# A rotary embedding on one core: all of x loaded early as fp16, with rows of 8 KB instead of 4 KB in loads and stores

## The chip, the cores and the metric

One core of a Trainium2 chip. The metric is the device time of one execution in microseconds, read as a median of several runs. "Span" is the time from the first to the last instruction in a profile; the device time is 1.7 to 2.2 us longer. All times inside a run are counted from the first instruction of its span.

## The reference

```python
# x: (8, 8, 1024, 64) float32; freqs: 32; positions: 0..1023; scale: 0.5
angles = np.outer(positions * scale, freqs)          # (1024, 32)
cos, sin = np.cos(angles), np.sin(angles)
x_first, x_second = x[..., :32], x[..., 32:]
out = concatenate([x_first * cos - x_second * sin,
                   x_first * sin + x_second * cos], axis=-1)   # float32
```

16.8 MB are read and 16.8 MB written, all as float32. Inside the kernels x, the tables and the results are fp16, except for the first unit's x and the set-up, which are fp32.

## The kernel before

The 64 heads are cut into 16 units of 4 heads (1 MB in HBM). In a unit, two heads fill the 128 partitions (64 partitions each, 16 positions in a partition), twice. So one partition's piece is 16 x 64 floats: a row of 4 KB in HBM.

```python
PAIRS_PER_UNIT = 2; PREFETCH = 5; BUF_X = 7; BUF_O = 7; BUF_P = 3
HP = P // 2;  K = S // HP;  KD = K * D          # 64, 16, 1024

def unit_dram(t, u):
    return t.rearrange("(i r) n -> i (r n)", r=2)[
        u * PU : (u + 1) * PU, :].rearrange("i (p n) -> p i n", n=KD)

X0 = xin0.tile([P, PU, KD], FP32)
nc.sync.dma_start(out=X0, in_=unit_dram(xv, 0))          # the first unit, not cast
for u in (0, 1):
    nc.sync.dma_start(out=pos_i64[u * HP : (u + 1) * HP, :], in_=...)
...
def load_unit(u):                                        # fp32 in HBM -> fp16 in SBUF
    X = xin.tile([P, PU, KD], FP16, tag="X")
    nc.gpsimd.dma_start(out=X, in_=unit_dram(xv, u))
for u in range(1, min(1 + PREFETCH, NU)):
    load_unit(u)
...                                                      # set-up: tables of cos and sin, 128 x 512
for u in range(NU):
    if u + 1 + PREFETCH < NU:
        load_unit(u + 1 + PREFETCH)
    nc.vector.tensor_tensor(out=pc, in0=X, in1=cosT, op=ALU.mult)    # 128 x 2048
    nc.vector.tensor_tensor(out=ps, in0=X, in1=sinT, op=ALU.mult)
    nc.vector.tensor_tensor(out=ov_[:, :, 0:half], in0=pcv[:, :, 0:half],
                            in1=psv[:, :, half:D], op=ALU.subtract)  # 128 x 1024
    nc.vector.tensor_tensor(out=ov_[:, :, half:D], in0=psv[:, :, 0:half],
                            in1=pcv[:, :, half:D], op=ALU.add)
    nc.gpsimd.dma_start(out=unit_dram(ov, u), in_=OUT)   # fp16 in SBUF -> fp32 in HBM
```

## Time and profile before

| | before |
|---|---|
| device time, median (3 runs) | 87.17 us (87.07 to 87.43) |
| span of the profiled run | 85.4 us |
| busiest engine | VectorE, 61.4 us (72%) |
| rows moved by the GpSimd queue | 7,936 and 496 end records |
| DMAs issued by GpSimd | 15 loads, 16 stores |

How to read it: VectorE's share is an average over a kernel in which it neither starts first nor ends last. A row is one contiguous piece in HBM that one of the 16 DMA engines moves; an end record is the 4-byte record that each engine moves after its rows of one DMA. The line to read first is that of the DMA, and its GB/s count the destination's bytes, so a casting load shows half of what it reads. The prediction below shows these lines.

### The profile page before, as it was taken

To read this page: it belongs to the slowest core of one execution; us is meant where nothing else is said; L and a number is where in the kernel's file an instruction comes from. 1 tells how busy PE (TensorE), PEld (TensorE's weight loads), DVE (VectorE), ACT (ScalarE), POOL (GpSimd) and SP (SyncE) were. 2 spreads that over 40 slices of the span, in tenths; PEclk is the share of its full clock that TensorE was granted. 3 is DMA by queue.
4 is the path that set the end of the run, shared out by engine and by line. 5 is a ranking of instruction groups with operands and counts; after the bars stand their busy time and mean duration, and the time that the engine had idled before them with its cause. 6 is when DMAs were issued, how large, how long until landed. Compare 5 with 4: busy or idle time off the path is not lost.

```text
span 85.4 us, 193 instructions
## 1 busy us (share of the span) xinstructions
PE 0.6 (1%) x2; PEld 0.5 (1%) x2; DVE 61.4 (72%) x72; ACT 3.5 (4%) x5; POOL 22.6 (26%) x35
## 2 busy tenths in 40 slices
PE   0002000000000000000000000000000000000000
PEld 0002000000000000000000000000000000000000
DVE  0002979999999999999999999999995992000000
ACT  6000090000000000000000000000000000000000
POOL 4990000005306245063360630311303033000000
DMA  2799999999999999999999999999999999999960
GB/s 19 313 288 214 208 211 213 212 208 211 257 384 218 421 430 271 319 351 257 415 208 396 274 334 338 252 407 221 406 260 331 426 428 428 428 426 416 424 225 0
DMA packets 8867, 25.72 MB, mean 301 GB/s; under 512 B 674, under 2 KB 674, under 8 KB 8866
## 3 DMA queue, kind: packets, MB, share of 16 engines
q0 software_dynamic: 8432, 24.64, 107.0%
q1 hardware_dynamic: 434, 1.07, 3.7%
q14 instruction: 1, 0.01, 0.0%
HBM read 16.79 MB, written 16.78 MB: 393 GB/s over the span
## 4 chain that ended last, share of the span: by engine, by line
DVE 46%; issue 23%; DMA 7%; POOL 4%; ACT 1%; SPq 1%; POOLq 1%; DVEq 0%
DVE ps L139 16%; DVE pc L138 11%; DVE OUT L144 8%; DVE OUT L148 8%; DMA pos_i<-in_positions_dram 7%; POOL out_dram L153 4%; ACT tabs L120 1%; DVE m L114 1%; POOLq L184 1%; DVE y L102 1%; DVE rneg L116 1%; SPq L76 1%; SPq L71 1%; DVE yc L109 1%; DVE posf L97 0%
## 5 line engine op out<-in xcount | busy, mean ns | idle before, releaser
L153 POOL DMA_DIRECT2D out_dram<-OUT x16 | 11.5, 718 | 47.8 <-DVE OUT L148 47.8
L138 DVE TENSOR_TENSOR pc<-X,tabs 128x2048 f16<-128x2048 f16 (+1 forms) x16 | 20.5, 1284 | 1.6 <-DMA X<-in_x_dram 1.0
L139 DVE TENSOR_TENSOR ps<-X,tabs 128x2048 f16<-128x2048 f16 (+1 forms) x16 | 20.5, 1284 | 0.0
L90 POOL DMA_DIRECT2D X<-in_x_dram x15 | 10.9, 739 | 1.2 <-POOLq L170 0.8
L144 DVE TENSOR_TENSOR OUT<-pc,ps 128x1024 f16<-128x1024 f16 x16 | 10.9, 684 | 0.0
L148 DVE TENSOR_TENSOR OUT<-ps,pc 128x1024 f16<-128x1024 f16 x16 | 10.9, 683 | 0.0
L97 DVE CAST posf<-pos_i 128x16 f32<-128x16 int32 x1 | 0.2, 174 | 6.9 <-DMA pos_i<-in_positions_dram 6.9
L120 ACT ACTIVATE tabs<-rneg 128x512 f16<-128x512 f32 x4 | 2.2, 617 | 8.7 <-DVE rneg L116 8.7
L120 ACT ACT_TABLE_LOAD x1 | 1.3, 1283 | 0.7 <-PEq L170 0.7
L102 DVE TENSOR_TENSOR y<-posf,cfreq 128x512 f32<-128x512 f32 x1 | 0.7, 687 | 0.1
L84 DVE MEMSET coef<- 1x128 f32 x1 | 0.2, 165 | 0.8 <-PEq L170 0.8
L116 DVE SCALAR_TENSOR_TENSOR rneg<-m,yc 128x512 f32<-128x512 f32 x1 | 0.7, 685 | 0.0
L116 DVE SCALAR_TENSOR_TENSOR rneg<-m,y 128x512 f32<-128x512 f32 x1 | 0.7, 684 | 0.0
L86 PE MATMUL cfreq<-freq_row,coef 1*128 1x32 f32 x2 | 0.6, 391 | 7.3 <-DMA freq_row<-in_freqs_dram 7.3
L86 PEld LDWEIGHTS cfreq<-freq_row,coef 1*128 1x128 f32 x2 | 0.5, 304 | 7.3 <-issue 7.3
L114 DVE TENSOR_SCALAR m<-yc 128x512 f32<-128x512 f32 x1 | 0.4, 427 | 0.0
L109 DVE TENSOR_SCALAR yc<-y 128x512 f32<-128x512 f32 x1 | 0.4, 426 | 0.0
L114 DVE TENSOR_SCALAR m<-y 128x512 f32<-128x512 f32 x1 | 0.4, 422 | 0.0
L170 POOL MEMSET const-float32-0.0<- 128x1 f32 x1 | 0.1, 93 | 0.2 <-issue 0.2
L170 POOL MEMSET const-bfloat16-1.0<- 128x1 bf16 x1 | 0.1, 95 | 0.0
L170 POOL MEMSET const-float32-1.0<- 128x1 f32 x1 | 0.1, 93 | 0.0
L170 POOL MEMSET const-uint8-127<- 128x1 uint8 x1 | 0.1, 92 | 0.0
## 6 DMA issues: line engine op xcount, KB each, us to landing
out_dram<-OUT POOLq DMA_DIRECT2D x16, 1024.0 KB, 13.2
X<-in_x_dram POOLq DMA_DIRECT2D x15, 512.0 KB, 12.3
X<-in_x_dram SPq DMA_DIRECT2D x1, 1024.0 KB, 5.1
pos_i<-in_positions_dram SPq DMA_DIRECT2D x2, 8.0 KB, 5.3
freq_row<-in_freqs_dram SPq DMA_DIRECT2D x1, 0.1 KB
```

Source lines behind the costliest of these rows:

```text
L86: nc.tensor.matmul(out=cfreq, lhsT=coef, rhs=freq_row, start=True, stop=True)
L90: nc.gpsimd.dma_start(out=X, in_=unit_dram(xv, u))
L102: nc.vector.tensor_tensor(out=y, in0=posf.unsqueeze(2).broadcast_to((P, K, half)), in1=cfreq.unsqueeze(1).broadcast_to((P, K, half)), op=A ...
L109: nc.vector.tensor_scalar(out=yc, in0=y, scalar1=0.25, scalar2=None, op0=ALU.add)
L114: nc.vector.tensor_scalar(out=m, in0=src, scalar1=_MAGIC, scalar2=None, op0=ALU.add)
L116: nc.vector.scalar_tensor_tensor(out=rneg, in0=m, scalar=_MAGIC, in1=src, op0=ALU.subtract, op1=ALU.subtract)
L120: nc.scalar.activation(out=tabs[:, i, :, h * half : (h + 1) * half], in_=rneg, func=AF.Sin, bias=0.0, scale=-_TWO_PI_DN,)
L138: nc.vector.tensor_tensor(out=pc, in0=X, in1=cosT, op=ALU.mult)
L139: nc.vector.tensor_tensor(out=ps, in0=X, in1=sinT, op=ALU.mult)
L144: nc.vector.tensor_tensor(out=ov_[:, :, 0:half], in0=pcv[:, :, 0:half], in1=psv[:, :, half:D], op=ALU.subtract,)
L148: nc.vector.tensor_tensor(out=ov_[:, :, half:D], in0=psv[:, :, 0:half], in1=pcv[:, :, half:D], op=ALU.add,)
L153: nc.gpsimd.dma_start(out=unit_dram(ov, u), in_=OUT)
```

## The change

Its intent: longer rows (fewer, larger pieces for the DMA), loads out of the way of the stores (all of x stays in SBUF as fp16), fewer DMAs. The arithmetic of a unit is the same.

```diff
-PAIRS_PER_UNIT = 2; PREFETCH = 5; BUF_X = 7; BUF_O = 7
+GROUPS = (1, 1, 2, 2, 3, 3, 3)
+BUF_O = 10
-    HP = P // 2
+    HEADS = 4
+    HP = P // HEADS                       # 32 positions per partition: rows of 8 KB
     K = S // HP
+    xv = x.rearrange("b h s d -> (b h s d)").rearrange("(u p n) -> p u n", p=P, n=N)
-        nc.sync.dma_start(out=pos_i64[...], ...)          # two
+        nc.scalar.dma_start(out=pos_i64[...], ...)        # four
-    for u in range(1, min(1 + PREFETCH, NU)):
-        load_unit(u)                                      # the others inside the loop
+    for g, n in enumerate(GROUPS):
+        X = xin.tile([P, n, N], FP16, name=f"X{g + 1}")
+        nc.gpsimd.dma_start(out=X, in_=xv[:, u0 : u0 + n, :])
-    tabs = consts.tile([P, 2, K, D], FP16)                # both halves written, 4 activations
+    cosT = consts.tile([P, K, half], FP16)                # one half, 2 activations,
+    sinT = consts.tile([P, K, half], FP16)                # read twice by a broadcast:
+    cos_b = cosT.unsqueeze(2).broadcast_to((P, K, 2, half))
+    sin_b = sinT.unsqueeze(2).broadcast_to((P, K, 2, half))
 ...
-        nc.gpsimd.dma_start(out=unit_dram(ov, u), in_=OUT)
+        nc.gpsimd.dma_start(out=ov[:, u, :], in_=OUT.rearrange("p k h j -> p (k h j)"))
```

## The prediction

> **What bounds the kernel now.** I read the page first (busy shares, slices, queues), then the stage windows, then the groups by shape, the waits, the order of time, and last the DMA records of the trace one by one.
>
> ```profile
> DVE  0002979999999999999999999999995992000000
> DMA  2799999999999999999999999999999999999960
> GB/s 19 313 288 214 208 211 213 212 208 211 257 384 218 421 430 271 319 351 257 415 208 396 274 334 338 252 407 221 406 260 331 426 428 428 428 426 416 424 225 0
> ...
> q0 software_dynamic: 8432, 24.64, 107.0%
> ...
> HBM read 16.79 MB, written 16.78 MB: 393 GB/s over the span
> ```
>
> VectorE has the largest busy share of the engines (72%), but it stops seven slices before the end. The DMA row is at 9 from the third slice to the 38th. The GB/s row counts the bytes on the destination side: a casting load lands half the bytes that it reads, so 211 there is 422 at HBM, and the stores show 426 to 428 directly. On the HBM side the rate is therefore the same, some 420 to 430, in load, mixed and store slices. That is the mark of a DMA bound kernel. The windows show its edges:
>
> ```profile
> 1.20:2.40 1.20, 0.00 (x0) 0.00 (x0) 0.00 (x0) 0.82 (x1) 1.13 (x2) 1.00 0.41 34
> 4.80:20.00 15.20, 0.60 (x2) 0.49 (x2) 11.37 (x14) 2.19 (x4) 2.34 (x4) 1.00 1.13 215
> 20.00:62.00 42.00, 0.00 (x0) 0.00 (x0) 42.00 (x49) 0.00 (x0) 14.38 (x20) 1.00 1.19 321
> 62.00:82.00 20.00, 0.00 (x0) 0.00 (x0) 7.88 (x10) 0.00 (x0) 2.15 (x3) 1.00 1.23 398
> 82.00:82.30 0.30, 0.00 (x0) 0.00 (x0) 0.00 (x0) 0.00 (x0) 0.00 (x0) 1.00 0.76 232
> 82.30:85.40 3.10, 0.00 (x0) 0.00 (x0) 0.00 (x0) 0.00 (x0) 0.00 (x0) 1.00 0.03 8
> ```
>
> The last two columns are DMA share and GB/s. The time has three parts: 2.4 us before the first load is at full rate, 79.9 us of full DMA (2.4 to 82.3), and 3.1 us of completion and closing. The median time of 87.17 is 1.8 us above the 85.4 span; I carry that 1.8 over.
>
> VectorE's work by shape, and the waits:
>
> ```profile
> L139 DVE TENSOR_TENSOR ps<-X,tabs 128x2048 f16<-128x2048 f16 x15 | 18.3, 1217 | 0.0
> L144 DVE TENSOR_TENSOR OUT<-pc,ps 128x1024 f16<-128x1024 f16 x16 | 10.9, 684 | 0.0
> L138 DVE TENSOR_TENSOR pc<-X,tabs 128x2048 f16<-128x2048 f32 x1 | 2.3, 2292 | 0.6 <-ACT tabs L120 0.6
> POOL out_dram L153 <- DVE OUT L148: 47.8, 16, 12.6
> DVE posf L97 <- DMA pos_i<-in_positions_dram: 6.9, 1, 6.9
> DVE pc L138 <- DMA X<-in_x_dram: 1.0, 1, 1.0
> ```
>
> In the order of time a unit takes 3.47 us (neighbours overlap, so less than 2 x 1.217 + 2 x 0.684). The 47.8 us that GpSimd waits for VectorE cost nothing: the DMA queue has work meanwhile. The last store is issued here:
>
> ```profile
> 71.19 0.72 POOL L153 DMA_DIRECT2D out_dram<-OUT  x1 [1.75 <-DVE OUT L148]
> ```
>
> In the DMA records the sixteenth store's first row moves only at 79.14 us, so it stood 8 us in the queue. VectorE has that much slack.
>
> **The DMA's cost of one row.** Taking all differences between start times of rows, one spacing stands out. In the store stage it is 153 ns (then 306, 459, 612), for 4 KB rows to HBM; in the load stage 154 ns (308, 462, 616); for the fp32 load from SyncE about 155.5. After every 16 rows of one DMA there is a 4-byte record, and spacings across it are 21 ns longer. So a unit's load costs 16 x 0.154 + 0.021 = 2.485 us and a store 16 x 0.153 + 0.021 = 2.469 us; the unit starts in the records show 2.48 and 2.47. Sum for the kernel: first load 16 x 0.1555 = 2.49, 15 loads 37.27, 16 stores 39.50, small constants 0.2, together 79.46 of the 79.9 us found. The rest is ramp and engines that end unevenly.
>
> **What the Trainium skill says.**
> (1) DMA: Bandwidth & Descriptors, "Where 436 GB/s comes from": the ceiling is 16 ports x 32 bytes x 850 MHz = 435 GB/s, and it says that for transfers with HBM its other limit, about 358, binds. The trace differs: 428 in store slices, so the first ceiling is the one met. At it, 4096 bytes are 128 beats or 150.6 ns; the 153 and 154 ns of the trace are 130 and 131 beats.
> (2) The same page, "Why small descriptors are slow (HBM only)": a fixed overhead of about 3 cycles for each packet, its example being a 256-byte descriptor. The 2 to 3 cycles that I find at 4 KB agree. This is what longer rows can save, so it is small.
> (3) The same page, "Issuing engines are not separate DMA queues": all DMAs run on the same 16 engines and interleave. The trace agrees (one total rate throughout), so moving the position loads to ScalarE and the order of loads and stores create no bandwidth.
> (4) Vector Engine (DVE) Microarchitecture Reference, "5.1 Performance modes": two elements per cycle need 16-bit operands with innermost step 1; a row read again and again with step 0 was tried and kept that rate. The trace has it for a broadcast of the outer dimension (1.217 us for 2048, against 2.29 with fp32) and for runs of 32 (0.684 for 1024), not yet for a broadcast in the middle.
>
> **The change part by part.**
> *Rows of 8 KB.* If the 2 and 3 cycles are paid once for each row, an 8 KB store row takes 256 + 2 cycles = 303.5 ns and a load row 256 + 3 = 304.7. A store becomes 8 x 0.3035 + 0.021 = 2.449, sixteen 39.18 (0.32 less). Loads: 15 units x 8 x 0.3047 = 36.56, and seven end records instead of fifteen, 0.15, together 36.71 (0.56 less). The first load 8 x 0.306 = 2.45 (0.04 less). Sum: **0.92 us off the DMA stage**, all of it on the path.
>
> *All loads early.* Seven GpSimd issues at 0.73 us each (now seven as well in the first 6.4 us). In the trace the queue serves loads and stores in order of issue (the first store moves at 22.08 us, after the seven loads ahead of it), so all loads go first, until about 2.4 + 2.45 + 36.7 = 41.6 us, then stores back to back. No byte is removed. The one load wait (1.0 us) goes, off the path: 0.
>
> *Set-up on VectorE and ScalarE.* 32 positions per partition instead of 16, so every table operation doubles to 128x1024: at one cycle per element the 0.69 us ones become 0.69 + 512/0.96 = 1.22, the 0.43 ones 0.43 + 256/0.96 = 0.69, an activation from 0.617 to about 1.04 (two instead of four). The chain from positions to first product grows from 4.0 us (7.84 to 11.88) to about 0.2 + 3 x 1.22 + 3 x 0.69 = 5.9. Positions on their own ScalarE queue should not stand behind all of the first load, which may return 1 to 3 us. First product between 10 and 14 us, then two fp32 products 4.4 + 1.2, then 15 x 3.47 = 52: VectorE ends at 68 to 72 us. Its sixteenth store is wanted at about 41.6 + 15 x 2.45 = 78.4. Off the path: 0.
>
> *Ten output buffers.* Unit 11 needs store 1 landed: about 41.6 + 2.45 + 2 = 46, while VectorE gets there at some 16 + 9 x 3.47 + 2 = 49 at the earliest. Later units only gain margin (2.45 against 3.47). When loads end, eight or so stores are queued, 20 us of work, and VectorE adds one each 3.47 us, so the queue lasts the eight remaining ones. No stall: 0.
>
> Sum: DMA ends at 82.3 - 0.9 = 81.4, span 84.5, time 87.17 - 0.9 = **86.3 us**, 1.0% less.
>
> **The rivals.**
> A. *Rows are cut at 4 KB inside the DMA*, so the overhead is paid as often as now. Then only eight end records go, 8 x 21 ns = 0.17 us: 87.0. No row of 8 KB of x is in this trace, so nothing speaks against it.
> B. *The overhead is hidden at 8 KB*, and the ceiling is met. Each engine moves 2.10 MB at 27.2 bytes per ns (the skill's ceiling / 16, an estimate) in 77.1 us, plus 0.5 of end records and 0.2 of constants: 77.8 instead of 79.46, so 85.5. Even this is 1.9% only, which is why I give "faster" little.
> C. *The middle broadcast loses the doubled rate.* A product then takes some 2.2 us, a unit 5.6, VectorE ends near 13 + 16 x 5.6 = 103, and the time is about 109, bound by VectorE. Against: the skill's note and the runs of 32 at 684 ns.
> D. *The start slips or engines end unevenly*: longer issues of 384 rows, or a queue that can't hold 1,920 rows at once. GpSimd works 5 us ahead of need, and landing times of up to 18.4 us (18.4 / 2.47 x 256 = some 1,900 rows) show that as many were held before. At worst some 1 us: 87 to 88.
>
> **Range and chances.** The sum gives 86.3; A and B bracket it at 87.0 and 85.5; the spread of before is 0.36. D widens the upper end. Range **85.3 to 87.4**. Faster by over 2% means below 85.43, beyond even B: 0.12. Slower by over 2% (above 88.9) needs C or a strong D: 0.07. Within 2%: 0.81.
>
> **What would show it.** Right: row spacings of about 303 to 305 ns in the DMA records (A: 306 to 308; B: 301); stores at 428 to 431 GB/s; slices at half of that until about 41 us and full after; products still at 1.217 us; GpSimd never waiting so long that the DMA row drops below 9 between 3 and 81 us; 3.1 us of closing. Wrong: a hole in the DMA row about 41 to 50 us (stores late), products at 2.2 us (C), or rows of 8 KB at another rate than these cycles, which would mean that I read a property of one row length as a cost of each row.

## The result, and the profile after

The changed kernel took 86.0 us (median of 4 runs, 85.94 to 86.14) beside 87.3 for before (87.07 to 87.72). The ratio is 0.986, 95% interval 0.982 to 0.990. A ratio here is the mean time of one kernel's runs over that of the other's of the same rounds, so it is not quite the ratio of the medians. Run again later with five rounds it was 0.984. So: 1.4 to 1.6% faster, 86.3 predicted.

First the page of the changed kernel: the slices of VectorE and DMA, the GpSimd queue, and the HBM bytes.

```profile
DVE  0000799999999999999999999999999999300000
DMA  2899999999999999999999999999999999999970
GB/s 31 331 280 212 212 216 216 216 210 216 216 214 210 216 216 216 212 214 218 171 418 432 436 424 412 432 432 428 428 428 436 420 412 436 436 424 432 428 284 0
...
q0 software_dynamic: 4336, 24.64, 99.1%
...
HBM read 16.81 MB, written 16.78 MB: 399 GB/s over the span
```

The same bytes move in half the rows (4,336 records are 3,968 rows and 368 end records, against 8,432). The row of GB/s has lost its alternation: half-value slices (loads) up to the twentieth, then full ones (stores). The DMA row still stands at 9 from the third to the 38th slice. One slice is low, 171, at the change from loads to stores.

Then the windows of the changed kernel (the last two columns are DMA share and GB/s):

```profile
1.20:2.40 1.20, 0.00 (x0) 0.00 (x0) 0.00 (x0) 0.00 (x0) 1.16 (x2) 1.00 0.64 102
4.80:20.00 15.20, 0.60 (x2) 0.50 (x2) 11.19 (x11) 2.11 (x2) 1.30 (x2) 1.00 1.06 214
20.00:40.00 20.00, 0.00 (x0) 0.00 (x0) 20.00 (x24) 0.00 (x0) 3.28 (x6) 1.00 1.07 215
40.00:42.00 2.00, 0.00 (x0) 0.00 (x0) 2.00 (x4) 0.00 (x0) 0.00 (x0) 1.00 1.06 174
42.00:60.00 18.00, 0.00 (x0) 0.00 (x0) 18.00 (x22) 0.00 (x0) 2.95 (x6) 1.00 1.12 426
60.00:80.00 20.00, 0.00 (x0) 0.00 (x0) 12.27 (x15) 0.00 (x0) 2.38 (x5) 1.00 1.12 428
81.50:84.20 2.70, 0.00 (x0) 0.00 (x0) 0.00 (x0) 0.00 (x0) 0.00 (x0) 1.00 0.02 6
```

VectorE's groups by shape, a wait, and the last store's issue in the order of time:

```profile
L128 DVE TENSOR_TENSOR pc<-X,cosT 128x2048 f16<-128x2048 f16 x15 | 18.2, 1216 | 0.0
L132 DVE TENSOR_TENSOR OUT<-pc,ps 128x1024 f16<-128x1024 f16 x16 | 10.9, 681 | 0.0
...
DVE posf L90 <- DMA pos_i<-in_positions_dram: 7.0, 1, 7.0
...
72.60 0.53 POOL L138 DMA_DIRECT2D out_dram<-OUT  x1 [1.93 <-DVE OUT L135]
```

The product with a broadcast in the middle takes 1,216 ns, as the one without did (1,217). VectorE now ends later than before, its last store issued at 72.60 instead of 71.19 us, and the kernel ends sooner. That is what "not the bound" looks like.

Where the 1.3 us went, by the two traces. The start and end of the DMA's work are taken from its records, row by row:

| | before | after | difference |
|---|---|---|---|
| first row of the GpSimd queue starts | 5.05 | 4.95 | -0.10 |
| from there to the end of the last row | 77.89 | 77.17 | -0.72 |
| from there to the end of the span | 2.44 | 2.10 | -0.34 |
| device time less span (means of the runs) | 1.94 | 1.77 | -0.17 |

In sum -1.33. The first line is about as large as its scatter (4.88 to 5.00 in six traces of kernels with this start). The third is far beyond its own (2.10 to 2.14 in the six traces with 23 GpSimd DMAs, 2.42 to 2.49 in the five with 31). The spans of before vary (84.9 to 86.0 in later runs), so that the sum holds for these two traces and not for every pair of runs. The windows show the ends, in before and then in the changed kernel (rows count where they start):

```profile
82.50:83.00 0.50, 0.00 (x0) 0.00 (x0) 0.00 (x0) 0.00 (x0) 0.00 (x0) 1.00 0.09 25
83.00:84.00 1.00, 0.00 (x0) 0.00 (x0) 0.00 (x0) 0.00 (x0) 0.00 (x0) 1.00 0.00 0
```
```profile
81.60:82.00 0.40, 0.00 (x0) 0.00 (x0) 0.00 (x0) 0.00 (x0) 0.00 (x0) 1.00 0.14 41
82.00:83.00 1.00, 0.00 (x0) 0.00 (x0) 0.00 (x0) 0.00 (x0) 0.00 (x0) 1.00 0.00 0
```

### The profile page after: what moved, and what is told of

Read it like the earlier page. It is cut to its first block, busy times and chain, and to the rows that moved or that the text cites. A ratio compares the mean times of both kernels' runs of the same rounds, so it can differ in the third digit from the quotient of the medians.

```text
span 84.2 us, 183 instructions
## 1 busy us (share of the span) xinstructions
PE 0.6 (1%) x2; PEld 0.5 (1%) x2; DVE 63.6 (76%) x72; ACT 3.4 (4%) x3; POOL 13.7 (16%) x27
## 3 DMA queue, kind: packets, MB, share of 16 engines
q0 software_dynamic: 4336, 24.64, 99.1%
## 4 chain that ended last, share of the span: by engine, by line
DMA 45%; issue 31%; POOL 10%; POOLq 1%
DMA X<-in_x_dram 45%; POOL out_dram L138 5%; POOL X L78 5%; POOLq L169 1%; POOLq L138 0%; POOLq L155 0%
## 5 line engine op out<-in xcount | busy, mean ns | idle before, releaser
L129 DVE TENSOR_TENSOR ps<-X,sinT 128x2048 f16<-128x2048 f16 (+1 forms) x16 | 20.5, 1282 | 0.0
L128 DVE TENSOR_TENSOR pc<-X,cosT 128x2048 f16<-128x2048 f16 (+1 forms) x16 | 20.4, 1282 | 0.0
L138 POOL DMA_DIRECT2D out_dram<-OUT x16 | 8.6, 538 | 58.4 <-DVE OUT L135 55.5
L78 POOL DMA_DIRECT2D X<-in_x_dram x7 | 4.9, 715 | 0.8 <-POOLq L155 0.8
L95 DVE TENSOR_TENSOR y<-posf,cfreq 128x1024 f32<-128x1024 f32 x1 | 1.2, 1220 | 0.8 <-PE cfreq L87 0.8
L119 ACT ACTIVATE sinT<-rnegs 128x1024 f16<-128x1024 f32 x1 | 1.1, 1057 | 8.8 <-DVE rnegs L109 8.8
L109 DVE SCALAR_TENSOR_TENSOR rnegs<-ms,y 128x1024 f32<-128x1024 f32 x1 | 1.2, 1219 | 0.0
L109 DVE SCALAR_TENSOR_TENSOR rnegc<-mc,yc 128x1024 f32<-128x1024 f32 x1 | 1.2, 1217 | 0.0
L117 ACT ACTIVATE cosT<-rnegc 128x1024 f16<-128x1024 f32 x1 | 1.1, 1057 | 0.1
L115 DVE TENSOR_SCALAR yc<-y 128x1024 f32<-128x1024 f32 x1 | 0.7, 693 | 0.0
```

What stands on the lines that cost most here:

```text
L78: nc.gpsimd.dma_start(out=X, in_=xv[:, u0 : u0 + n, :])
L95: nc.vector.tensor_tensor(out=y, in0=posf.unsqueeze(2).broadcast_to((P, K, half)), in1=cfreq.unsqueeze(1).broadcast_to((P, K, half)), op=A ...
L109: nc.vector.scalar_tensor_tensor(out=rneg, in0=m, scalar=_MAGIC, in1=src, op0=ALU.subtract, op1=ALU.subtract)
L117: nc.scalar.activation(out=cosT, in_=rc, func=AF.Sin, bias=0.0, scale=-_TWO_PI_DN)
L119: nc.scalar.activation(out=sinT, in_=rs, func=AF.Sin, bias=0.0, scale=-_TWO_PI_DN)
L128: nc.vector.tensor_tensor(out=pc, in0=X, in1=cos_b, op=ALU.mult)
```

## The experiments

The theory: the kernel is bound by the DMA, which pays 3.5 ns for each load row and 2.4 ns for each store row beside the bytes, so longer rows pay; loading early and VectorE's changes lie off the path. Rivals: the gain comes from the order (all loads before all stores); from the number of DMAs; or VectorE is nearer to the path than it looks.

### 1. Rows of 8 KB alone: rows8_inter

```diff
-    HP = P // 2
+    HP = P // 4                # and r=4, PAIRS_PER_UNIT = 1; all else as before
```

> The kernel before with the rows alone changed to 8 KB (4 heads in one set of rows, so 32 positions per partition and a doubled set-up); loads still one unit each, five ahead, mixed with the stores. Row theory (2 to 3 cycles per row, 21 ns per end record): loads 15 x (8 x 0.3047 + 0.021) = 36.88 instead of 37.27, stores 0.32 less, first load 0.04 less: 0.75 us below before, and up to 0.25 more if the first load's faster issue starts the DMA earlier. So a ratio to before of 0.989 to 0.991. Order theory (the gain comes from all loads going first): ratio 1.00.

Measured: 89.15 us, ratio 1.024 (1.021 to 1.027), slower by 2%. Both theories missed it. The DMA and GB/s rows of this kernel's page show why, and so do its windows:

```profile
DMA  1899999999279999999999999999999999999960
GB/s 23 342 273 212 214 212 210 214 212 210 56 301 301 259 425 412 199 400 265 344 323 282 381 233 427 226 402 269 336 329 276 432 425 432 447 421 421 428 229 0
...
21.00:22.00 1.00, 0.00 (x0) 0.00 (x0) 1.00 (x2) 0.00 (x0) 0.00 (x0) 1.00 1.03 209
22.00:23.00 1.00, 0.00 (x0) 0.00 (x0) 1.00 (x3) 0.00 (x0) 0.00 (x0) 1.00 0.37 70
23.00:24.00 1.00, 0.00 (x0) 0.00 (x0) 1.00 (x2) 0.00 (x0) 0.42 (x1) 1.00 0.00 0
24.00:25.00 1.00, 0.00 (x0) 0.00 (x0) 1.00 (x2) 0.00 (x0) 0.40 (x2) 1.00 0.45 180
```

In the eleventh slice the DMA has nothing to do. Seven loads were queued at the start (seven buffers) and they are done at 22.7 us. The next two jobs come only from VectorE: the first store, and the eighth load, which waits for VectorE to free a buffer. Rows of 8 KB double the set-up on VectorE (tables of 128x1024), so here these two are issued at 23.58 and 24.71 us. The hole, from 22.7 us to the first store's first row at 24.7, is 2.0 us, about what the kernel is slower. In the kernel before the first store was issued at 19.01, with the seven loads lasting until 22.9: it worked with some 3 us to spare.

### 2. The same with the hole closed: rows8_deep

```diff
-PREFETCH = 5
-BUF_X = 7
+PREFETCH = 9
+BUF_X = 11                 # on top of rows8_inter
```

> As rows8_inter (8 KB rows, loads of one unit mixed with stores, doubled set-up), but with 11 input buffers and nine loads ahead instead of 7 and five. In rows8_inter the DMA row had a hole of some 2.5 us at 22 to 25 us: its seven loads were done before the late first store and the eighth load (which waits for VectorE to free a buffer) were issued. Theory: that hole alone hid the gain; with eleven loads queued (4.6 + 11 x 2.44 = 31.4 us, first store at 24) it closes, and the rows give 0.75 to 1.0 us below before: ratio 0.988 to 0.991. Rival (8 KB rows are of use only with all loads first): ratio 1.00 or more.

Measured: 86.87 us, ratio 0.998 (0.995 to 1.001). The hole is gone, as the DMA row of its page shows below, and 2.3 us with it, so it was the cause of experiment 1. But the gain that the rows should give is only 0.2 of 0.75 us. In its trace the stage of the GpSimd queue (from its first row to the end of its last) lasts 77.42 us, against 77.89 in the profiled run of before: part of the gain is there. The rest is not accounted for in full. Between 24 and 34 us, around the first stores, a row takes some 322 ns of an engine's time instead of 307 to 308: 0.5 us lost. Before has such a patch too, with 0.24 us by the same count (see experiment 7), so some 0.25 us of the shortfall lie there. The profiled run of before was also slower than before usually is in these rounds (a span of 85.4 us against a median of 85.0), so its stage overstates what there was to gain. The number of DMAs explains nothing here: both kernels have 31 on GpSimd. What mixing loads and stores adds of itself stays open.

```profile
DMA  2799999999999999999999999999999999999960
```

### 3. The early loads alone: rows4_early

```diff
-    for u in range(1, min(1 + PREFETCH, NU)):
-        load_unit(u)
+    for g, n in enumerate((1, 1, 2, 2, 3, 3, 3)):     # rows of 4 KB, set-up as before
+        X = xin.tile([P, n * PU, KD], FP16, name=f"X{g + 1}")
+        nc.gpsimd.dma_start(out=X, in_=unit_dram(xv, u0, n))
```

> The kernel before with the early loads alone (x resident, 7 grouped loads before all stores, 10 output buffers), rows still 4 KB, set-up and position loads as before. Row theory: only eight end records go, 0.17 us, ratio 0.998. Order theory: the whole gain of the change, ratio 0.986.

Measured: 86.82 us, ratio 0.997 (0.994 to 1.000). As the row theory has it: -0.2 us. Its stage in the records lasts 77.90 us, the same as before's; the close is shorter (2.14 against 2.44), and so is the part outside the span (1.76 against 1.94). Both are told of in experiment 6. So the order by itself moves nothing. The step from here to the changed kernel, rows of 8 KB with early loads, is 0.8 us (86.82 to 86.0, in different rounds), as the rows' 0.75 predict.

### 4. The cost of a row by its length: rows2_inter, rows16_early

```diff
-    HP = P // 2                # before
+    HP = P // 1                # rows2_inter: rows of 2 KB, four sets of rows in a unit
```
```diff
-    HEADS = 4                  # changed kernel
+    HEADS = 8                  # rows16_early: rows of 16 KB, units of 2 MB, the last in two halves
```

> The kernel before with rows of 2 KB (one head in a set of rows, four sets in a unit). Row theory: a load row 64 + 3 cycles = 78.8 ns, 32 in a unit, so 0.056 us more for each of 15 loads (0.84); a store row 64 + 2 cycles, 0.038 more for each of 16 stores (0.60); first load 0.06: 1.5 us above before, ratio 1.017. Order theory: ratio 1.00. More than 1.03 would mean that something else than rows comes in, such as GpSimd's longer issues (512 rows a unit) or a full queue.

> The changed kernel with rows of 16 KB (8 heads in one set, 8 units of 2 MB, the last unit computed and stored in two halves of 8 KB rows). Row theory: half of the remaining row cost goes (60 load rows x 3.5 ns = 0.21, about 60 store rows x 2.35 ns = 0.14) and nine end records (0.19): some 0.5 us below the changed kernel, ratio to before 0.980. Rival: the set-up on VectorE doubles again, so the last store is issued later than the queue wants it, and 0.5 to 2 us are lost: ratio 0.986 to 1.00, with a hole in the DMA row before the last store.

Measured: 89.58 us for 2 KB (ratio 1.029) and 95.63 for 16 KB (1.097). Neither time is the row theory's. The 16 KB kernel's rival named the reason but not the size: it expected 0.5 to 2 us lost, and 9.6 were. And yet these runs measure the row. From the spacings of row starts in the DMA records, over stretches in which the queue is full, in ns (bytes alone: an estimate, the row at 32 bytes per cycle of 850 MHz, from the Trainium skill's ceiling that the prediction cites):

| row in HBM | bytes alone | load row | over | store row | over |
|---|---|---|---|---|---|
| 2 KB | 75.3 | 78.8 | 3.5 | 77.7 | 2.4 |
| 4 KB | 150.6 | 154.2 | 3.6 | 153.0 | 2.4 |
| 8 KB | 301.2 | 304.7 | 3.5 | 303.5 | 2.3 |
| 16 KB | 602.4 | 605.9 | 3.5 | 604.7 | 2.3 |

The excess does not depend on the length. The prediction took it from a single length; this was its riskiest step, and it holds.

What else was in the times: with 2 KB rows 1.5 of the 2.5 us lost are the rows'. Of the other 1.0 some 0.6 lie at 7 to 12 us, where the loads run below their rate (148 GB/s at 8 to 9 us instead of 205). The cause was not looked for. With 16 KB rows VectorE waits 15.3 us for the positions instead of 7.0, as the waits of rows16_early show:

```profile
DVE posf L92 <- DMA pos_i<-in_positions_dram: 15.3, 1, 15.3
```

The tables then end late, VectorE issues its last store at 86.12 us, and the DMA row of this kernel's page has holes from the twenty-first slice on:

```profile
DMA  5699999999999999999929929829859659899991
```

The Trainium skill, page DMA: Bandwidth & Descriptors, section "Queues, rings and completion order", says that each engine goes round-robin between the queues that it has work for, a whole packet at a time. If longer rows make longer turns, a small record of the positions waits longer at each. This fits the waits (5.4, 6.9, 7.0 and 15.3 us for rows of 2, 4, 8 and 16 KB), but no run shows the turns, and the number of position loads changed along (1, 2, 4, 8), as did their queue (SyncE's in the first two, ScalarE's in the others). So it is not shown.

rows16_mixed tried to save the 16 KB rows: the first two units in halves of 8 KB rows, so that the positions land earlier.

```diff
+    for u, h in ((0, 1), (1, 0), (1, 1)):       # (0, 0) comes in fp32 from SyncE
+        nc.gpsimd.dma_start(out=XH, in_=xv[:, u, h * H : (h + 1) * H])
+    GROUPS = (1, 2, 3)                          # units 2 to 7 in rows of 16 KB
```

> The 16 KB layout with its first two units loaded in halves of 8 KB rows (the first half in fp32), and the last unit stored in halves. Row theory: against the changed kernel some 48 load rows per engine fewer (0.17 us), some 48 store rows fewer (0.11), five end records fewer (0.10): about 0.4 us below it, 85.6 or a ratio to before of 0.981. This needs the position loads by some 10 us (15.3 in rows16_early). If the set-up still ends late, the queue runs dry before the last stores: ratio 0.99 to 1.04.

Measured: 87.7 us, ratio 1.008 (1.005 to 1.012). The wait for the positions was 9.3 us, as needed, but the quadrupled tables (an fp32 product of 128x2048 takes 2.29 us) still delayed VectorE, so that the last store was issued at 78.66 us, and the queue ran dry from about 67 us. The limit here is not the row but VectorE, late by the set-up that grows with it.

### 5. VectorE's slack: late4, late8

```diff
-    nc.vector.tensor_tensor(out=y, ...)
+    for _ in range(1 + 4):                      # late8: 1 + 8
+        nc.vector.tensor_tensor(out=y, ...)     # the same product again: VectorE later, nothing else
```

> The changed kernel with one set-up product computed four more times on VectorE, so everything on VectorE is some 4.6 us later. Theory of the slack: the last store is issued at 77.2 instead of 72.6, the queue wants it at about 78.7: +0 to +0.3 us. If VectorE were on the path: +4.6 us.

> The changed kernel with the set-up product computed eight more times: VectorE some 9.1 us later, the last store issued at 81.7, moved about 1.5 us later, 2.45 us long, 2.4 us of closing: span 88.0 against 84.2, so 3.8 us above the changed kernel, ratio to before 1.03. With late4 (no loss at 4.6 us) this would place the slack at about 5.5 us. If the queue feeds from a deeper reserve than I think: less.

Measured: late4 85.98 us (ratio 0.988), no loss for a VectorE that runs over 5 us later. late8 90.36 us (1.034), 4.3 us above the changed kernel of the same rounds (3.8 expected). The last store's issue in the order of time, in late4 and then in late8:

```profile
77.69 0.53 POOL L139 DMA_DIRECT2D out_dram<-OUT  x1 [1.93 <-DVE OUT L136]
```
```profile
82.67 0.53 POOL L139 DMA_DIRECT2D out_dram<-OUT  x1 [1.93 <-DVE OUT L136]
```

In late8 the last row ends at 86.37 us, 3.7 us after that issue, with the store before it just done. In the changed kernel the last row ends at 82.12, so an issue up to 82.12 - 3.7 = 78.4 costs nothing. It issues at 72.60: a slack of 5.8 us. late4 uses 5.1 of it, late8 overdraws it by 4.3, and that is what late8 lost.

### 6. The number of DMAs: after_again, loads15, pairs

```diff
-GROUPS = (1, 1, 2, 2, 3, 3, 3)
+GROUPS = (1,) * 15                              # loads15
```
```diff
-GROUPS = (1, 1, 2, 2, 3, 3, 3)
+GROUPS = (1, 2, 4, 8)                           # pairs: 4 loads
+        if u % 2 == 0:
+            OUT2 = xout.tile([P, 2, K, 2, half], FP16, name="O", tag="O")
+        OUT = OUT2[:, u % 2]                    # one store for two units;
+        ...                                     # the last two units each by itself: 9 stores
```

> The changed kernel once more, beside the next three on the same chip: 86.0, ratio to before 0.986 to 0.988.

> The changed kernel with its fifteen loads on GpSimd issued one by one, still all early. Row theory: eight more end records of 21 ns, 0.17 us above the changed kernel (86.2, ratio to before 0.989). Rival (the number of DMAs has a larger cost, at the close or outside the span, which would explain why the 8 KB rows mixed with stores gained only 0.2 us of 0.75): 0.4 to 0.7 us above it. Order alone (the mixing itself costs the rest): 0.1 to 0.2 us.

> A candidate to beat both: the changed kernel with loads of 1, 2, 4 and 8 units and with seven stores of two units (2 MB) and two of one: ten DMAs fewer. Ten end records of 21 ns: 0.21 us below the changed kernel, 85.8. If the number of DMAs has a larger cost, 0.4 to 0.8 us below it.

Measured, in the same rounds:

| kernel | GpSimd DMAs | device time (range) | ratio to before (interval) | end of last row to end of span |
|---|---|---|---|---|
| loads15 | 31 | 86.35 (86.28 to 86.46) | 0.988 (0.985 to 0.991) | 2.42 |
| after_again | 23 | 86.05 (85.78 to 86.28) | 0.984 (0.980 to 0.987) | 2.11 |
| pairs | 13 | 85.43 (85.33 to 85.69) | 0.978 (0.975 to 0.981) | 1.73 |

Eight DMAs more cost 0.30 us, ten fewer save 0.62: 0.04 to 0.06 us each, two to three times the 21 ns of an end record. Most of it is in the close. From the end of the last row to the end of the span it takes 2.42 to 2.49 us in five traces with 31 GpSimd DMAs, 2.10 to 2.14 in six with 23, 1.96 with 17 (rows16_mixed), 1.81 with 14 (rows16_early) and 1.73 with 13: about 0.04 us for each DMA, whatever the rows. In the traces it is GpSimd's last DRAIN instruction that ends later, 1.66, 1.35 and 0.98 us after the last row in the three; why, the profile doesn't show.

The end records are harder to see. The stage is 77.13, 77.38 and 77.14 us in the three, but it holds a slow patch (experiment 7) of 0.15, 0.69 and 0.49 us. Without it 77.0, 76.7 and 76.6 are left (an estimate): the order that the end records ask for (0.17 and 0.21 us apart), with one trace for each. The part outside the span was 1.95, 1.79 and 1.76 us (means of device time less span); it does not follow the number of DMAs alone, for rows16_early has 2.17 with 14. pairs beats both kernels; it is the best version found, 2.2% below before, with an interval that leaves it open whether the 2% are reached.

### 7. The slow patch between loads and stores: touch_out

In the changed kernel's records, 33 load rows that start between 40.3 and 41.9 us, just ahead of the first store, take 0.35 to 0.72 us instead of 0.32. Over all engines that is 6.4 us, 0.4 us of the stage (divided by 16, an estimate), and it is the slice of 171 GB/s above. In before 18 load rows are slow in the same way just ahead of its first store, which moves at 22.7 us.

```diff
+    zero = consts.tile([16, half], FP32)
+    nc.vector.memset(zero, 0.0)
+    nc.scalar.dma_start(out=ov[0:16, 0, 0:half], in_=zero)    # written over by the first store
```

> The changed kernel with a tiny early write (16 rows of 128 bytes of zeros) to the first unit's output, written over later. In the trace of the changed kernel 33 load rows just ahead of the first store take 0.1 to 0.4 us longer than the others, 6.4 engine-us in all, 0.4 us of the DMA stage. If that is the cost of the first write to the output, it goes or moves to the start of the kernel: up to 0.4 us less. Otherwise it stays, and the time is the same.

Measured: 86.15 us, ratio 0.990 (0.986 to 0.994), and the patch is there as before (40 rows, 7.5 us over all engines; 175 GB/s in the same slice). A first write to the output is not its cause, at least not one to these 16 rows. The cause stays open.

## Why the prediction was right or wrong, point by point

**DMA bound: right.** late4 shows it most plainly: VectorE 5 us later, the same time. Loads run at 214 to 215 GB/s in the windows before and after, stores at 426 to 428 in the windows after and at 416 to 428 in the slices before, and the bytes did not change.

**The cost of a row: right, and the core of it.** 304.7 and 303.5 ns were predicted for a length that the trace did not hold, and measured; at 2 and 16 KB the excess is the same. Rival A (rows cut at 4 KB: 306 to 308) and rival B (no excess at 8 KB: 301) are both out.

**The size of the stage's gain: 0.92 predicted, about 0.7 measured.** What the sum lacked is the slow patch at the change from loads to stores: 0.40 us in the changed kernel, 0.26 in before (excess over the usual duration, all rows, divided by 16: an estimate). Without it the stage is 77.6 us before and 76.7 to 76.8 after. That is 0.9 less, what the rows and the eight end records promised. rows4_early, where only the end records go, has 77.5 on the same terms. The patch is not the same in every run (0.15 to 0.69 us in the changed kernel and its variants), and so the measured gain of a single pair of traces can't be trusted to better than some 0.2 us.

**Start and close carried over unchanged: wrong in size.** The prediction took 3.1 us of closing from a window that started too soon (the last row ends at 82.9, not 82.3, so it was 2.4), and then gave the changed kernel the same. Measured 2.1, with 0.15 to 0.2 less outside the span; the traces of experiment 6 tie the close to the number of DMAs. The start came about 0.1 us sooner, hardly more than its scatter. These three terms, 0.6 us in the traces at hand and less beside a typical run of before (rows4_early, with the same 23 DMAs, gained 0.2 to 0.3 us in all), are what the prediction lacked. They more than made up for the patch. That 86.3 came so near to 86.0 is therefore in part luck: one missing cost and some missing gains.

**All loads early, "off the path, 0": right for 4 KB rows (rows4_early: -0.2 us, by the close), but too narrow.** Its worth is in what it makes harmless. With 8 KB rows and seven buffers the doubled set-up opens a hole of 2 us (rows8_inter). The prediction treated the parts as a sum of independent terms; two of them need one another.

**Set-up and VectorE: right to within half a microsecond.** First product at 14.4 us (predicted 10 to 14), VectorE's end at 72.3 (68 to 72). The positions' own queue brought less than the 1 to 3 us guessed: VectorE waits 7.0 us for them, against 6.9 in before with shorter rows and 7.7 to 7.8 in rows8_inter and rows8_deep, which have the same rows and the same four loads on SyncE. The broadcast in the middle kept the doubled rate (rival C out: 1,216 ns). The 0.96 elements per ns in its sums fit the trace of before, whose fp32 products take 687 ns for 512 elements and 2,292 for 2,048.

**Buffers and queue (rival D): right.** No digit of the DMA row falls below 9 from the third to the 38th slice; the patch at 41 us shows in the GB/s alone.

**Two times read too early.** The prediction has the first store's first row at 22.08 us and the sixteenth's at 79.14. On the clock of the views they are 22.70 and 79.76. Nothing in its sum rests on them.

## What to carry to other kernels

When the DMA row is full from start to end, work out what a row costs beside its bytes and how many rows there are; that product is all that longer rows can give (here 0.75 of 79 us), and it can be predicted from the spacings in the trace (0.9 us predicted for rows and end records, 0.7 measured, 0.9 without the slow patch). Before lengthening rows, ask what grows with them: here the set-up on VectorE doubled, which is free only with enough loads queued to cover it (rows8_inter lost 2%), and at 16 KB not even then. After rows, count DMAs: each one less saved 0.04 to 0.06 us here.

## What the Trainium skill lacked or had wrong

- DMA: Bandwidth & Descriptors, "Why small descriptors are slow": about 3 cycles for each packet. The runs show 3.5 ns (3 cycles of 850 MHz) for a casting load row and 2.4 ns (2 cycles) for a casting store row, the same from 2 to 16 KB. The page's example stops at small descriptors and does not tell loads from stores.
- DMA: Bandwidth & Descriptors, "Where 436 GB/s comes from": it says that the HBM side (about 358) binds for transfers with HBM. Taken alone the sentence misleads, as the page's own 425 GB/s for a 16 MB load by one core shows. The runs add stores: 426 to 428 GB/s at HBM were held for whole stages of casting stores.
- DMA: Bandwidth & Descriptors gives a fixed cost of a DMA by itself. No page has what one more GpSimd DMA adds to the end of a kernel, after the last row has landed: about 0.04 us, from 1.73 us with 13 DMAs to 2.42 with 31.
- No page has the slow patch where loads give way to stores: 33 rows of 8 KB, 0.4 us of the stage in the changed kernel, 0.15 to 0.69 in its variants, cause open.
- The round-robin between queues ("Queues, rings and completion order") comes without a figure for small loads beside long rows: VectorE waited 5.4 us for the positions with 2 KB rows and 15.3 with 16 KB rows (with 1 and 8 position loads).
